# Sums moved into adding DMAs: seven weight pairs a layer and five squares of the MLP's norm in a two-layer decoder trunk

## The chip, the cores and the metric

The kernel runs on one core of a Trainium2 chip. The metric is the device time of one execution in microseconds. The engines are named as in the profile: PE (TensorE: matmuls, with its weight loads listed as PEld), DVE (VectorE), ACT (ScalarE), POOL (GpSimd) and SP (SyncE, which here issues DMAs and nothing else). A `q` behind an engine's name is its queue, the part that waits and issues.

## The reference

A trunk of two layers on 512 tokens of width 1024, in float32. Cut to what matters here:

```python
def hybrid_layer(x, g_mix, w_in, sinks, w_a, w_b, w_out, g_mlp, w_up, w_down):
    h = rmsnorm(x, g_mix)
    z = h @ w_in
    ...
    ya = sliding_window_sink_attention(aq, ak, av, sinks) @ w_a
    ...
    yb = r.astype(x.dtype) @ w_b
    mixed = jax.nn.sigmoid(ga) * ya + jax.nn.sigmoid(gb) * yb
    x = x + mixed @ w_out
    h2 = rmsnorm(x, g_mlp)
    x = x + jnp.square(jax.nn.relu(h2 @ w_up)) @ w_down
    return x
```

`rmsnorm` divides by the root of the mean of the squares over the 1024 features. `r` is the output of a retention with four heads. A last norm follows the second layer.

## The kernel before

**Layout.** Activations are kept transposed: features on the 128 partitions, the 512 tokens along the free dimension, so a tensor of width 1024 is eight tiles of 128 x 512. The residual `x` stays in SBUF as such eight tiles.

**Three matmuls for one.** PE multiplies in a reduced float32 format. To keep the precision each operand is split into a high part (ACT copies it into the format, L255 for weights, L308 and L311 for activations) and a low part (DVE subtracts the high part, L256, L309, L312). A product is then high by high, high by low and low by high (`products`, L301 to L303; `wide_pair` puts two of them into one matmul of 512 columns, L1259, and the third into L1260).

**Weights.** They come from DRAM in units of 128 x 1024 in one fixed order (`unit_order`). `load_until` issues the loads on SP's queue into `raw` tiles, of which there are three; `split_until` makes the high and low halves, three of each; `unit` hands them to the matmuls and keeps the splitting three units ahead of PE. A load waits until its `raw` tile is free.

**Pairs.** Most of `w_b`, `w_out` and `w_up` is multiplied in a form with seven block products in place of eight, in the manner of Strassen and Winograd: two units (two rows of the stacked weights, here `one` and `two`) become four parts, and parts 0 to 2 hold sums and differences of halves of 128 x 512. `load_part` issues the loads of a pair: for part 0 the left half of `one` (L210) and all of `two` (L212, into the `raw` tile that later serves part 3), for part 1 the right half of `one` (L215). `add_part` forms the sums on DVE: for part 0 the right half becomes the sum of the two halves of `two` (L221), for part 1 L224, for part 2 L228 and L229. The activations get the same treatment (`sum_input`, L559 to L563). A layer has 19 pairs: two in `w_b`, three in `w_out`, fourteen in `w_up`. `narrow_pair` multiplies with 256 columns a matmul and moves partial sums with ACT (L595, L598, L602); `wide_pair` is used for `w_up` from unit 6 on.

**The norm of the MLP.** In the out-projection the first two tiles of `x` come from `two_chunks`, the other six from three pairs. When a tile is done, `next_input` scales and splits it (L311, L312) and adds its squares up (`squared_input`, `square_sum`): the first square goes straight into the accumulator `acc` (L391), each of the seven that follow is made by ACT in a temporary (L394) and added by DVE (L395). Temporaries of that tag are six. During the first group of `w_up` the sum is split (`sum_parts`, the tiles `sh` and `sl`), multiplied with ones on PE (L430) and turned into the factor `rstd` (L431, L432), which the results of `w_up` are multiplied with.

**Order.** Each engine works through its instructions in a fixed order. The order is planned when the program is built, by a scheduler that goes through the code's order and lets an instruction pass that cannot start yet by its own model of time; a few places fix the order by hand (`issue_after`). Where instructions fall away or come in, the plan is made anew.

Of the kernel before, what the change touches and what calls it, by code (L numbers as in the profile page):

```python
# [13 lines left out]
AF = mybir.ActivationFunctionType  # L14
ALU = mybir.AluOpType
# [6 lines left out]
KD = D // P  # L22
# [35 lines left out]
def unit_order():  # L58

    def plain(name, *at):  # L60
        return [(name, i) for i in range(*at)]

    def pairs(src, *firsts):
        return [("pair", j, part, src) for j in firsts for part in range(4)]

    order = plain("w_in", 26) + plain("w_a", 4) + plain("w_in", 26, 46)
    order += pairs("w_b", 0, 2) + plain("w_b", 4, 8)
    order += plain("w_out", 2) + pairs("w_out", 2, 4, 6)
    for what, q, i in mlp_sequence():
        if what == "first":  # L70
            order += plain("w_up", 4)
        elif what == "pair":
            order += pairs("w_up", 8 * q + 2 * i)
        elif what == "down":
            order += plain("w_down", 8 * q + 2 * i, 8 * q + 2 * i + 2)
        else:
            order += plain("w_down", 8 * q, 8 * q + 8)
    return order
# [48 lines left out]
def decoder(ctx, tc, xT, x_first, w_in, w_a, w_b, w_out, w_up, w_down, tables, decay, band, triangles, g_last, out):  # L127
    nc = tc.nc
# [13 lines left out]
    def temp(name="t"):  # L142
        return tmp.tile([P, T], F32, tag="t", name=name)

    def big(name, dtype=F32):
        return tmp.tile([P, 2, T], dtype, tag="big", name=name, bufs=7)
# [13 lines left out]
    x = little_x[:, P:].rearrange("p (k t) -> p k t", t=T)  # L160
# [4 lines left out]
    order = [(layer, *u) for layer in range(DEPTH) for u in unit_order()]  # L165
    raws, parts, homes = {}, {}, []
# [8 lines left out]
    def raw_tile():  # L175
        return wpool.tile([P, UNIT], F32, tag="raw", name="raw")
# [8 lines left out]
    def load_until(n):  # L185
        while state["loaded"] < min(n, len(order)):
            i = state["loaded"]
            layer, name, j = order[i][:3]
            if name == "pair":
                load_part(i)  # L190
            else:
                raws[i] = raw_tile()
                for at in halves(i):
                    queue = nc.scalar if i == 0 and at.start == 0 else nc.sync
                    queue.dma_start(raws[i][:, at], weights[name][layer, j][:, at])
                    if i < 3:
                        load_x()
            state["loaded"] += 1
# [3 lines left out]

    LEFT, RIGHT = slice(0, UNIT // 2), slice(UNIT // 2, UNIT)

    def load_part(i):
        layer, _, j, part, src = order[i]
        one, two = (weights[src][layer, j + a] for a in range(2))
        if part == 0:
            raws[i] = raw_tile()
            nc.sync.dma_start(raws[i][:, LEFT], one[:, LEFT])  # L210
            raws[i + 3] = raw_tile()
            nc.sync.dma_start(raws[i + 3], two)  # L212
        elif part == 1:
            raws[i] = big("raw2").rearrange("p a t -> p (a t)")
            nc.sync.dma_start(raws[i][:, RIGHT], one[:, RIGHT])  # L215

    def add_part(i):
        part = order[i][3]
        if part == 0:
            w2 = raws[i + 3]  # L220
            nc.vector.tensor_tensor(raws[i][:, RIGHT], w2[:, RIGHT], w2[:, LEFT], ALU.add)  # L221
        elif part == 1:
            w1 = raws[i - 1]
            nc.vector.tensor_tensor(raws[i][:, LEFT], w1[:, RIGHT], w1[:, LEFT], ALU.subtract)  # L224
        elif part == 2:
            raws[i] = big("raw3").rearrange("p a t -> p (a t)")
            w1, w2, z2 = raws[i - 2], raws[i + 1], raws[i - 1]
            nc.vector.tensor_tensor(raws[i][:, LEFT], w1[:, LEFT], w2[:, RIGHT], ALU.subtract)  # L228
            nc.vector.tensor_tensor(raws[i][:, RIGHT], z2[:, RIGHT], z2[:, LEFT], ALU.subtract)  # L229

    def split_until(n):
        while state["split"] < min(n, len(order)):
            i = state["split"]
            load_until(i + 3)
            paired = order[i][1] == "pair"
            if paired:
                add_part(i)
            raw = raws[i]
            if homes and i >= len(order) - len(homes):
                home = homes[len(order) - 1 - i]  # L240
                hi, lo = (home[:, 2 * a : 2 * a + 2, :].rearrange("p a t -> p (a t)") for a in range(2))
            else:


                first = (ASIDE, ASIDE) if paired else (0, 0)
                if paired and order[i][4] == "w_up" and wide(order[i][2]):
                    first = (ASIDE, 0)
                hi, lo = (
                    wpool.tile([P, UNIT + P], F32R, tag=n, name=n)[:, a : a + UNIT] for n, a in zip(("hi", "lo"), first)
                )  # L250
            for at in (LEFT,) if paired and order[i][3] == 3 else halves(i):
                if i == 0 and at.start == 0:
                    nc.vector.tensor_copy(hi[:, at], raw[:, at])
                else:
                    nc.scalar.activation(hi[:, at], raw[:, at], AF.Copy)  # L255
                last_low[:] = [nc.vector.tensor_tensor(lo[:, at], raw[:, at], f32(hi[:, at]), ALU.subtract).ins]  # L256
            raws.pop(i - 3 if paired else i, None)
            parts[i] = (hi, lo)
            state["split"] += 1
# [129 lines left out]
    def square_sum(acc, src, first):  # L389
        if first:  # L390
            nc.scalar.activation(acc, src, AF.Square)  # L391
        else:
            sq = temp("sq")
            nc.scalar.activation(sq, src, AF.Square)  # L394
            nc.vector.tensor_tensor(acc, acc, sq, ALU.add)  # L395
# [38 lines left out]
    acc_of = {}  # L434

    def scaled_input(k, which):

        split(*xs[k], x[:, k, :], gain[:, which * KD + k : which * KD + k + 1])

    def squared_input(k, which):  # L440
        if k == 0:
            acc_of[which] = tmp.tile([P, T], F32, tag="acc", name="acc", bufs=1)
        square_sum(acc_of[which], x[:, k, :], k == 0)

    class Rms:

# [89 lines left out]
    def layer_body(layer):  # L536
        g_mix, g_mlp = 2 * layer, 2 * layer + 1
# [116 lines left out]
        def squares():  # L654
            for k in range(KD):
                squared_input(k, g_mix)
# [420 lines left out]
        for u in range(4):  # L1077
            hi, lo = unit("w_a", layer)
            for j in range(2):
                c = 2 * u + j  # L1080
# [103 lines left out]

        def next_input(c):
            scaled_input(c, g_mlp)
            squared_input(c, g_mlp)

        def put_x(c):
            def put(ps):  # L1190
                nc.vector.tensor_tensor(x[:, c, :], x[:, c, :], ps, ALU.add)
                next_input(c)

            return put
# [15 lines left out]
        for c in range(2, KD, 2):  # L1210
            pool = ps_mm if c == 4 else ps_aux
            narrow_pair(pool, lambda ins: None, form_of(by_form_m), block_m, add_to_x(c))
            for i in range(2):
                next_input(c + i)
# [122 lines left out]
        def put_down(c, last=False):  # L1337
            def put(ps):
                nc.vector.tensor_tensor(x[:, c, :], x[:, c, :], ps, ALU.add)  # L1339
                if last:  # L1340
                    scaled_input(c, g_mix + 2)
                    squared_input(c, g_mix + 2)
                    nc.sync.dma_start(spill[:, c, :], x[:, c, :])

            return put
# [216 lines left out]
```

## Time and profile before

| | |
|---|---|
| median of 3 runs | 1479.97 us (1479.74 to 1479.98) |
| the profiled execution | 1481.1 us, its span 1478.5 us |
| mean granted PE clock | 0.999 |
| DMA | 166.13 MB, mean 112 GB/s, queue of SP 34.9% of 16 engines' span |
| L395, adds of squares | 28 instructions of 685 ns |
| L394, squares | 28 instructions of 619 ns |

The span runs from the first to the last instruction; what lies around it in the profiled execution is 1481.1 - 1478.5 = 2.6 us. A row of a timeline gives the start and the duration in us, the engine, the line, the operation, the tile written and those read, the shapes, and in brackets the idle time before it and what ended it. A row of a group gives the count, the busy time, the mean of one in ns and the idle time before. Weight units are used in this order within layer 0: `w_b` from about 319 us, `w_out` from 360, `w_up` from 404; layer 1 does the same 732 us later.

### The profile page before, as it was taken

What the parts mean: (1) busy time and instruction counts of PE and PEld (TensorE: products, weight loads), DVE (VectorE), ACT (ScalarE), POOL (GpSimd) and SP (SyncE); (2) the same over time, 40 slices, a digit from 0 to 9 for tenths busy, and PEclk for the clock granted to TensorE, in tenths of its full rate; (3) what the DMA queues carried; (4) which work ended last, traced back from release to release, by engine and by line L of the source; (5) the groups of instructions that cost most, each with busy time, mean ns of one, the idle gap of its engine ahead of it and who ended that gap; (6) DMA issues with size and microseconds to landing.
All of it is one profiled execution on the core that took longest, in us unless ns stands there. A gap on an engine that the chain in (4) does not pass through costs nothing.

```text
span 1478.5 us, 20008 instructions
## 1 busy us (share of the span) xinstructions
PE 1467.9 (99%) x7466; PEld 1249.9 (85%) x7466; DVE 1162.7 (79%) x1920; ACT 810.3 (55%) x1302; POOL 3.8 (0%) x14
## 2 busy tenths in 40 slices
PE   9999999999999999999999999999999999999998
PEld 7888888888988888888888888888889888888887
DVE  7998668778998787776678975686889977878763
ACT  7656356654674445444556743656547654444553
POOL 0000000000000000000000000000000000000000
PEclk9999999999999999999999999999999999999999
DMA  6422223246323333333543232323553323333241
GB/s 226 135 87 86 93 82 104 93 164 191 102 79 114 100 114 94 106 100 115 170 128 91 85 98 89 99 92 98 175 167 104 101 97 99 115 101 112 89 141 57
DMA packets 56945, 166.13 MB, mean 112 GB/s; under 512 B 6896, under 2 KB 7056, under 8 KB 56848
## 3 DMA queue, kind: packets, MB, share of 16 engines
q1 hardware_dynamic: 56560, 164.33, 34.9%
q8 instruction: 58, 0.95, 0.3%
q10 hardware_dynamic: 288, 0.52, 0.1%
q14 instruction: 39, 0.32, 0.1%
HBM read 153.80 MB, written 8.40 MB: 110 GB/s over the span
## 4 chain that ended last, share of the span: by engine, by line
PE 86%; DVE 6%; issue 6%; DMA 1%; ACT 0%; POOLq 0%; DVEq 0%; SPq 0%
PE mm L303 20%; PE mm L301 20%; PE mm L302 20%; PE mm L1259 10%; PE mm L1260 5%; DVE lo L256 2%; PE rv L301 2%; PE rv L302 2%; PE rv L303 2%; DVE r L309 1%; PE score L797 1%; PE r L301 1%; PE r L303 1%; PE r L302 1%; DMA inv<-row 0%
## 5 line engine op out<-in xcount | busy, mean ns | idle before, releaser
L302 PE MATMUL mm<-r,hi 128*128 128x512 f32 (+1 forms) x1568 | 572.7, 367 | 0.0
L301 PE MATMUL mm<-r,hi 128*128 128x512 f32 (+1 forms) x1568 | 570.6, 368 | 1.4 <-ACT eu L598 0.7
L303 PE MATMUL mm<-r,lo 128*128 128x512 f32 (+1 forms) x1568 | 563.1, 367 | 1.6 <-DVE lo L256 1.3
L255 ACT ACTIVATE hi<-raw 128x1024 fp32r<-128x1024 f32 (+1 forms) x334 | 334.4, 1003 | 393.1 <-PE mm L302 210.9
L256 DVE TENSOR_TENSOR lo<-raw,hi 128x512 fp32r<-128x512 f32 (+1 forms) x335 | 385.2, 1152 | 118.8 <-ACT hi L255 115.7
L303 PEld LDWEIGHTS mm<-r,lo 128*128 128x128 f32 x1568 | 293.3, 188 | 51.1 <-DVE lo L256 3.7
L301 PEld LDWEIGHTS mm<-r,hi 128*128 128x128 f32 x1568 | 294.0, 188 | 50.2 <-ACT eu L598 1.5
L302 PEld LDWEIGHTS mm<-r,hi 128*128 128x128 f32 x1568 | 294.3, 188 | 45.7
L1259 PE MATMUL mm<-r,hi 128*128 128x512 f32 x728 | 251.9, 391 | 0.0
L1260 PE MATMUL mm<-r,lo 128*128 128x256 f32 x728 | 200.4, 277 | 1.2 <-DVE lo L256 1.1
L1259 PEld LDWEIGHTS mm<-r,hi 128*128 128x128 f32 x728 | 136.5, 188 | 28.3
L1260 PEld LDWEIGHTS mm<-r,lo 128*128 128x128 f32 x728 | 136.6, 188 | 5.2 <-DVE lo L256 2.7
L1339 DVE TENSOR_TENSOR x<-x,mm 128x512 f32<-128x512 f32 x56 | 37.8, 687 | 29.2 <-PE mm L303 29.2
L1332 ACT ACTIVATE z<-z 128x512 f32<-128x512 f32 x56 | 32.5, 624 | 48.3 <-DVE z L1312 48.3
L302 PE MATMUL rv<-lo,r 128*128 128x512 f32 x128 | 49.8, 389 | 0.0
L303 PE MATMUL rv<-hi,r 128*128 128x512 f32 x128 | 49.5, 389 | 0.0
L301 PE MATMUL rv<-hi,r 128*128 128x512 f32 x128 | 49.4, 390 | 0.0
L308 ACT ACTIVATE r<-z 128x512 fp32r<-128x512 f32 x64 | 38.7, 621 | 12.6 <-DVE z L1022 12.5
L309 DVE TENSOR_TENSOR r<-z,r 128x512 fp32r<-128x512 f32 x64 | 43.1, 686 | 2.8 <-ACT r L308 2.6
L824 ACT ACTIVATE sm<-sm,st 128x256 f32<-128x256 f32 (+1 forms) x64 | 30.2, 474 | 19.1 <-DVE st L812 18.9
L1312 DVE SCALAR_TENSOR_TENSOR z<-z,rstd 128x512 f32<-128x512 f32 x52 | 35.7, 687 | 0.6
L221 DVE TENSOR_TENSOR raw<-raw 128x512 f32<-128x512 f32 x38 | 26.0, 684 | 7.0 <-DMA raw<-w_up_in 6.3
(261 smaller groups left out, 1693.0 us busy)
## 6 DMA issues: line engine op xcount, KB each, us to landing
raw<-w_in_in SPq DMA_DIRECT2D x89, 512.0 KB, 3.6
raw<-w_down_in SPq DMA_DIRECT2D x64, 512.0 KB, 3.6
raw<-w_up_in SPq DMA_DIRECT2D x36, 512.0 KB, 3.6
raw<-w_up_in SPq DMA_DIRECT2D x56, 256.0 KB, 2.8
raw<-w_b_in SPq DMA_DIRECT2D x12, 512.0 KB, 4.0
raw<-w_out_in SPq DMA_DIRECT2D x10, 512.0 KB, 7.1
raw<-w_a_in SPq DMA_DIRECT2D x8, 512.0 KB, 3.5
aside<-gb SPq DMA_DIRECT2D x8, 512.0 KB, 4.7
```

Source lines behind the costliest of these rows:

```text
L255: nc.scalar.activation(hi[:, at], raw[:, at], AF.Copy)
L256: last_low[:] = [nc.vector.tensor_tensor(lo[:, at], raw[:, at], f32(hi[:, at]), ALU.subtract).ins]
L301: nc.tensor.matmul(ps, ah, bh, start=start and i == 0, stop=False, **more)
L302: nc.tensor.matmul(ps, ah, bl, start=False, stop=False, **more)
L303: nc.tensor.matmul(ps, al, bh, start=False, stop=stop and i == n - 1, **more)
L308: nc.scalar.activation(hi, src, AF.Copy)
L309: nc.vector.tensor_tensor(lo, src, f32(hi), ALU.subtract)
L1259: nc.tensor.matmul(both, hi[:, c], m, start=start and k == 0, stop=False, **more)
L1260: nc.tensor.matmul(ps[:, :H], lo[:, c], m[:, 0, :], start=False, stop=k == 3 and start, **more)
L1312: nc.vector.scalar_tensor_tensor(z[:, :, at], z[:, :, at], 0.0, factor, ALU.max, ALU.mult)
L1332: nc.scalar.activation(z[:, i, :], z[:, i, :], AF.Square)
L1339: nc.vector.tensor_tensor(x[:, c, :], x[:, c, :], ps, ALU.add)
```

## The change

In `load_part` a pair is `summed` when it belongs to `w_b` or `w_out`, or to `w_up` with a first unit below 8: two, three and two, seven a layer. For a summed pair SP loads the right half of `two` into the right half of part 0's tile as well, and POOL then issues a DMA that loads the left half of `two` and adds it to what is there. `add_part` does nothing for part 0 of such a pair. All of `two` is loaded as before, for parts 2 and 3.

For the MLP's norm the squares of tiles 1 to 5 are made by ACT as before and added to `acc` by DMAs that POOL issues, from SBUF to SBUF. The square of tile 6 is kept, the square of tile 7 is added to it by DVE, and that sum to `acc`.

```diff
+    def summed(i):
+
+        _, _, j, _, src = order[i]
+        return src != "w_up" or j < 8
+
     def load_part(i):
         layer, _, j, part, src = order[i]
         one, two = (weights[src][layer, j + a] for a in range(2))
@@
             nc.sync.dma_start(raws[i][:, LEFT], one[:, LEFT])
             raws[i + 3] = raw_tile()
             nc.sync.dma_start(raws[i + 3], two)
+            if summed(i):
+                nc.sync.dma_start(raws[i][:, RIGHT], two[:, RIGHT])
+                nc.gpsimd.dma_start(raws[i][:, RIGHT], two[:, LEFT], accum_op=ALU.add)
         elif part == 1:
             raws[i] = big("raw2").rearrange("p a t -> p (a t)")
             nc.sync.dma_start(raws[i][:, RIGHT], one[:, RIGHT])
@@ def add_part(i):
         if part == 0:
             w2 = raws[i + 3]
+            if summed(i):
+                return
             nc.vector.tensor_tensor(raws[i][:, RIGHT], w2[:, RIGHT], w2[:, LEFT], ALU.add)
@@
-    def squared_input(k, which):
+    def squared_input(k, which, by_dma=False):
         if k == 0:
             acc_of[which] = tmp.tile([P, T], F32, tag="acc", name="acc", bufs=1)
-        square_sum(acc_of[which], x[:, k, :], k == 0)
+        acc = acc_of[which]
+        if not by_dma or k == 0:
+            square_sum(acc, x[:, k, :], k == 0)
+        elif k < KD - 2:
+            sq = temp("sq")
+            nc.scalar.activation(sq, x[:, k, :], AF.Square)
+            nc.gpsimd.dma_start(acc, sq, accum_op=ALU.add)
+        elif k == KD - 2:
+            acc_of["last"] = temp("sq")
+            nc.scalar.activation(acc_of["last"], x[:, k, :], AF.Square)
+        else:
+            last = acc_of.pop("last")
+            square_sum(last, x[:, k, :], False)
+            nc.vector.tensor_tensor(acc, acc, last, ALU.add)
@@
         def next_input(c):
             scaled_input(c, g_mlp)
-            squared_input(c, g_mlp)
+            squared_input(c, g_mlp, True)
```

## The prediction

> **What bounds the kernel now.** I read the page first, for the engine that sets the time.
>
> ```profile
> span 1478.5 us, 20008 instructions
> ...
> PE 1467.9 (99%) x7466; PEld 1249.9 (85%) x7466; DVE 1162.7 (79%) x1920; ACT 810.3 (55%) x1302; POOL 3.8 (0%) x14
> ...
> PE 86%; DVE 6%; issue 6%; DMA 1%; ACT 0%; POOLq 0%; DVEq 0%; SPq 0%
> ```
>
> TensorE (PE) is busy for 99% of the span. VectorE (DVE) has 79% and only 6% of the chain that ended last, but that share may sit in one place, and the change takes work from DVE alone. So the second view is the busy time of each engine by stretches, over the part of layer 0 in which the edited lines run (the sum also holds the same five stretches of layer 1, 732 us later).
>
> ```profile
> 300.00:340.00 40.00, 39.72 (x249) 35.52 (x248) 34.52 (x50) 23.05 (x34) 0.00 (x0) 1.00 0.52 171
> 340.00:380.00 40.00, 39.63 (x211) 34.08 (x211) 36.03 (x49) 19.24 (x26) 0.00 (x0) 1.00 0.53 171
> 380.00:400.00 20.00, 19.33 (x162) 18.90 (x160) 19.43 (x31) 13.20 (x22) 0.00 (x0) 1.00 0.26 80
> ...
> 430.00:450.00 20.00, 19.39 (x118) 16.63 (x118) 19.71 (x34) 14.12 (x23) 0.00 (x0) 1.00 0.34 108
> ...
> sum 300.00, PE 295.79 PEld 261.91 DVE 276.88 ACT 181.90 POOL 0.00; mean PE 29.58 PEld 26.19 DVE 27.69 ACT 18.19 POOL 0.00
> ```
>
> The columns are PE, PEld, DVE, ACT and POOL busy, the granted clock, the DMA share and GB/s. From 380 to 400 and from 430 to 450 DVE is as full as PE (19.43 and 19.71 of 20), and PE has its holes there. All holes of both layers together are 300.00 - 295.79 = 4.21 us. Who PE waits for, over the whole span:
>
> ```profile
> PE mm L303 <- DVE lo L256: 1.3, 2, 0.7
> PE mm L1260 <- DVE lo L256: 1.1, 3, 0.5
> ...
> PE mm L301 <- ACT eu L598: 0.7, 2, 0.4
> PE mm L301 <- ACT eu L602: 0.5, 2, 0.3
> ```
>
> So what can be won is a few us: waits for the low half of a weight unit (DVE), and waits for ACT, which the change does not relieve. The sizes here are too small, because the modelled end of a matmul covers part of each wait. The starts in PE's timeline give the full price:
>
> ```profile
> 337.38 0.40 PE L301 MATMUL mm<-r,hi 128*128 128x512 f32 x1
> 337.62 0.40 PE L302 MATMUL mm<-r,hi 128*128 128x512 f32 x1
> 338.10 0.50 PE L303 MATMUL mm<-r,lo 128*128 128x512 f32 x1
> ...
> 391.12 0.28 PE L301 MATMUL mm<-r,hi 128*128 128x256 f32 x1
> 391.23 0.28 PE L302 MATMUL mm<-r,hi 128*128 128x256 f32 x1
> 392.18 0.38 PE L303 MATMUL mm<-r,lo 128*128 128x256 f32 x1 [0.67 <-DVE lo L256]
> 392.40 0.28 PE L301 MATMUL mm<-r,hi 128*128 128x256 f32 x1
> ...
> 434.29 0.40 PE L1259 MATMUL mm<-r,hi 128*128 128x512 f32 x1
> 435.16 0.38 PE L1260 MATMUL mm<-r,lo 128*128 128x256 f32 x1 [0.47 <-DVE lo L256]
> ```
>
> A 256-wide matmul is followed after 0.11 us (391.12 to 391.23), a 512-wide one after 0.24 (337.38 to 337.62). So the stop at 391 costs 392.18 - 391.23 - 0.11 = 0.84, and 0.11 more as the next start is also late (392.40): 0.95. The stop at 434 costs 435.16 - 434.29 - 0.24 = 0.63, with the same aftermath 0.74. The stop at 337 costs 0.24 and 0.11: 0.35. These three are what DVE makes PE lose; each opens with the matmul that needs a low half.
>
> **What the change removes.** Seven pairs a layer lose the DVE add of part 0 (L221), five squares a layer lose theirs (L395). The last two squares keep two adds between them, as before.
>
> ```profile
> L221 DVE TENSOR_TENSOR raw<-raw 128x512 f32<-128x512 f32 x38 | 26.0, 684 | 7.0 <-DMA raw<-w_up_in 6.3
> ...
> L395 DVE TENSOR_TENSOR acc<-acc,sq 128x512 f32<-128x512 f32 x28 | 19.2, 685 | 0.0
> ```
>
> That is 24 instructions of 0.68 us, 16.4 us of DVE in the program. What counts is where they stand in DVE's order ahead of the three stops:
>
> ```profile
> 325.39 0.69 DVE L221 TENSOR_TENSOR raw<-raw 128x512 f32<-128x512 f32 x1
> ...
> 386.24 0.69 DVE L221 TENSOR_TENSOR raw<-raw 128x512 f32<-128x512 f32 x1
> ...
> 387.50 0.69 DVE L395 TENSOR_TENSOR acc<-acc,sq 128x512 f32<-128x512 f32 x1
> ...
> 390.30 0.69 DVE L395 TENSOR_TENSOR acc<-acc,sq 128x512 f32<-128x512 f32 x1
> 390.91 1.22 DVE L256 TENSOR_TENSOR lo<-raw,hi 128x1024 fp32r<-128x1024 f32 x1
> ...
> 428.87 0.63 DVE L221 TENSOR_TENSOR raw<-raw 128x512 f32<-128x512 f32 x1
> ```
>
> An add holds DVE's next instruction back by 0.61 us (390.30 to 390.91). The stop at 391 waits for the low half begun at 390.91. Three of the removed adds stand directly ahead of it, 1.83 us. Its other input, the high half, comes from ACT:
>
> ```profile
> 388.29 1.06 ACT L255 ACTIVATE hi<-raw 128x1024 fp32r<-128x1024 f32 x1
> ```
>
> It ends at 389.35, so the low half can begin 1.56 us earlier, more than the 0.95 of the stop: all of it goes. Ahead of the stop at 434 DVE has no gap from the reciprocal (it ends as L221 begins at 428.87) and one removed add: 0.6 of the 0.74 goes. Ahead of the stop at 337 one removed add, at 325.39, in a run of DVE without a gap longer than 0.5: all of 0.35. Sum: 0.95 + 0.6 + 0.35 = 1.9 us a layer, **3.8 us** in both.
>
> **What it adds.** Per pair, SP issues one 256 KB load more (the right half of the second row), and POOL then issues a 256 KB load that adds onto it. Per square, POOL issues a 256 KB transfer from SBUF to SBUF that adds onto the running sum. POOL has nothing else to do (14 instructions). The new wait stands on POOL's queue: an adding transfer waits until the right half has landed, or until the sum before it has, and behind it wait only other adding transfers. The trace shows no adding transfer and none issued by POOL. From issue to landing call it A. The nearest rows are the ordinary loads by SP, first of the page, then of the tensor w_out in the crowded stretch:
>
> ```profile
> raw<-w_up_in SPq DMA_DIRECT2D x56, 256.0 KB, 2.8
> ...
> DMA to landing us min/median/max: 3.2/7.2/7.3
> ```
>
> From below A is 2.8, one ordinary load. From above 14.6: twice 7.3, since an adding transfer reads two things, each as slowly as the slowest row. Nothing excludes the far end, but none of the waits falls in the crowded stretch except w_out's first pair, so I take 5.6, twice the ordinary load. [...]
>
> Where must it land? The tightest pair is the third of w_out, whose loads SP issued like this:
>
> ```profile
> 376.92 0.33 SPq L210 DMA_DIRECT2D raw<-w_out_in  x1
> 377.30 0.42 SPq L215 DMA_DIRECT2D raw<-w_out_in  x1
> 382.35 0.33 SPq L212 DMA_DIRECT2D raw<-w_out_in  x1
> ```
>
> L212, the whole second row, stands before L215 in the program and yet was issued after it, because it needs a buffer that comes free later. So SP's order lets work pass a load without a buffer, and the new load, which writes the same buffer as L210, should go out at 377.3 and land at 380.1. Without any stop at 391 the high half has to begin by 388.9 (0.95 before 390.91, less its own 1.06). So A may be 8.8, and 5.6 fits. The sum also no longer waits for L212's row. The extra traffic, 0.5 MB a pair, meets a DMA share of 0.53 at most, and PE's holes were not in the stretch where it is highest.
>
> The squares form a chain, since each must wait for the one before:
>
> ```profile
> 398.25 0.62 ACT L394 ACTIVATE sq<-x 128x512 f32<-128x512 f32 x1
> ...
> 414.97 0.68 DVE L395 TENSOR_TENSOR acc<-acc,sq 128x512 f32<-128x512 f32 x1
> ...
> 421.51 0.39 PE L430 MATMUL ssq<-sh,ones 128*128 128x512 f32 x1
> ```
>
> Four of the five come between ACT's squares ahead of 387.50 and the one that ends at 398.87. With A of 5.6 the second to fifth end no later than 398.87 + 2 x 5.6 = 410.1, before the final add at 414.97. The last two squares now make two adds in a row there, 0.61 longer; PE asks for the sum at 421.51, and between lie only the split's copy and one subtraction (some 2 us), so it is hidden. If the chain ran to 419.5, that cover would be gone. Squares stay on ACT, and their buffers are held longer, at most three of the six of that tag at once.
>
> **Sum.** The profiled span 1478.5 less 3.8 is 1474.7. Around the span lay 2.6 us (the profiled execution took 1481.1), so 1477.3 for an execution like it; the median of the three runs, 1479.97, lies 1.1 below that execution, so **1476.2**.
>
> **Rivals.** *More than the three stops.* With DVE freer, ACT's work moves forward too, and the waits for eu go as well. For it: DVE is nearly full wherever PE has holes. The ceiling is the 4.21 us of holes, plus 0.27 that each of about 18 stops hides behind the modelled ends and in the late start after it: 9 us. Against it: ACT's burst of squares and scalings is not touched. With two thirds of the ceiling, 6 us: 1474.
>
> *The gain is hidden or given back.* The order on each engine is planned anew when instructions fall away, and a stop filled at 391 may open elsewhere: PE has nothing to spare at 99%. For it: the stops are all under 1 us, so one instruction ordered otherwise costs as much as was won. With half of it lost: 1478; with all, 1480. [...]
>
> *The adding transfers land too late: slower.* One mechanism, the chain of squares in the out-projection. Its second to fifth link start no earlier than 386.2 (the add of the second ran at 387.50) and end at 386.2 + 4 A. It decides from A = (419.5 - 386.2) / 4 = 8.3 on, and every us of A above that stops PE for 4 us in each layer, since the matmul with ones at 421.51 holds all of PE's queue. At A = 10 that is 6.7 a layer, 13 in all, less what is won elsewhere, 3: 1490. The same point decides for the pair at 391 (8.8). For it: two reads for one write, and the w_out rows of 7.2. Against it: 2.8 in the uncrowded stretch, where this chain runs (DMA share 0.26).
>
> *The right half's load goes out behind L212 and not before.* Then it lands at 382.7 + 2.8 = 385.5, only 3.4 remain for A, and with 5.6 the stop at 391 is 2.2 long in place of 0.95. Against it speaks the order of L215. 1480 to 1482; I count it to the given-back cases.
>
> **How the numbers follow.** Chances: forecast 0.52 (its own range 1474 to 1478.5), more 0.10, hidden or given back 0.23, too late 0.15. About 0.2%, 3.0 us, is what a measurement of this kernel can tell from no change. Faster by more than that means under 1477.0: all of *more* and 0.40 of the forecast, 0.50. Slower, over 1482.9: all of *too late* and 0.02 of the given-back cases, 0.17. Within: 0.33. The range from 1473 to 1482 leaves out most of *too late* and the best part of *more*.
>
> **What would show it.** Right: L221 counts 24, L395 with the new add 18, DVE busy near 1146; POOL issues 24 transfers that land in under 8 us; the stops at 337 and 391 are gone in both layers and the one at 434 is below 0.2; the new load is issued next to L210. Wrong: PE waits at the matmul with ones or for a high half that waits for a POOL transfer (too late); DVE instructions longer than 0.69 beside POOL's issues (held); three stops gone and new ones of the same size elsewhere (given back).

## The result and the profile after

The changed kernel takes 1499.97 us (median of 4 runs, 1498.68 to 1501.05), the kernel before, timed beside it, 1479.89 (1479.74 to 1479.98). The ratio is 1.0135, with a 95% interval from 1.0118 to 1.0153: **20.1 us slower**. The forecast was 1476.2 with a range to 1482.

Line numbers are those of the changed kernel from here on. L265 is ACT's copy of a weight unit to its high half and L266 DVE's low half (L255 and L256 before); L311 to L313 are the three products (L301 to L303 before), L319 makes the low half of an activation, L322 that of a tile of `x`, and L618, L621 and L625 are ACT's copies of partial sums (L595, L598 and L602 before).

The page of the changed kernel, with the busy time of the engines, the chain that ended last by engine, and one costly group:

```profile
span 1499.3 us, 20085 instructions
...
PE 1474.6 (98%) x7466; PEld 1254.2 (84%) x7466; DVE 1150.0 (77%) x1896; ACT 809.3 (54%) x1302; POOL 24.7 (2%) x38
...
PE 80%; DVE 7%; issue 7%; DMA 5%; ACT 1%; SPq 0%; POOLq 0%; DVEq 0%
...
L234 DVE TENSOR_TENSOR raw<-raw 128x512 f32<-128x512 f32 x38 | 26.1, 687 | 22.6 <-DMA raw<-w_out_in 12.0
```

DVE lost the 24 instructions (1920 to 1896) and 12.7 us of work. What is new is the share of DMA in the chain, 1% before and 5% now, and the last row. L234 is the subtraction that makes part 1 of a pair (L224 before, with no idle time ahead of it). It reads both halves of part 0's tile, the sum among them, and DVE now stands idle 22.6 us ahead of it. Two lists of waits show the same from both ends. First, the waits of DVE and ACT for a load of weights that POOL had part in (engine, line, what it waited for: us in total, times, longest):

```profile
ACT hi L265 <- DMA raw<-w_out_in: 12.1, 2, 6.1
DVE raw L234 <- DMA raw<-w_out_in: 12.0, 4, 3.5
...
DVE raw L234 <- DMA raw<-w_up_in: 10.4, 4, 3.7
```

Second, what PE waited for:

```profile
PE mm L311 <- ACT eu L621: 6.4, 5, 2.4
PE ssq L440 <- DVE sl L319: 5.0, 2, 2.7
PE mm L313 <- DVE lo L266: 2.1, 3, 1.0
PE mm L1282 <- ACT hi L265: 1.8, 2, 0.9
```

No row of PE's waits names a DMA: PE waits for ACT's copies and for the split of the norm's sum, and the two largest rows are traced below to what stands in a queue behind the waiting subtraction. The busy time in the stretches that the prediction looked at (PE, PEld, DVE, ACT, POOL, granted clock, DMA share, GB/s):

```profile
380.00:400.00 20.00, 17.56 (x146) 17.36 (x147) 16.50 (x26) 11.80 (x20) 3.89 (x5) 1.00 0.73 171
...
430.00:450.00 20.00, 16.81 (x111) 15.58 (x110) 18.50 (x24) 13.42 (x23) 0.00 (x0) 0.91 0.18 58
```

From 380 to 400 DVE fell from 19.43 to 16.50, as was meant, but PE fell with it, from 19.33 to 17.56. This is that place in the changed kernel, from SP's, POOL's, DVE's, ACT's and PE's timelines in turn, for the third pair of `w_out`:

```profile
379.98 0.33 SPq L215 DMA_DIRECT2D raw<-w_out_in  x1
380.36 0.42 SPq L219 DMA_DIRECT2D raw<-w_out_in  x1
```

```profile
384.66 0.86 POOL L220 DMA_DIRECT2D raw<-w_out_in  x1 [3.46 <-DVE raw L238]
```

```profile
385.63 1.22 DVE L266 TENSOR_TENSOR lo<-raw,hi 128x1024 fp32r<-128x1024 f32 x1
389.98 0.69 DVE L234 TENSOR_TENSOR raw<-raw 128x512 f32<-128x512 f32 x1 [3.13 <-DMA raw<-w_out_in]
390.59 0.41 DVE L1222 TENSOR_TENSOR x<-x,mm 128x256 f32<-128x256 f32 x1
```

```profile
391.03 0.72 ACT L321 ACTIVATE r<-x 128x512 fp32r<-128x512 f32 x1 [2.57 <-DVE x L1222]
...
392.18 0.36 ACT L621 ACTIVATE eu<-mm 128x256 f32<-128x256 f32 x1
```

```profile
390.23 0.28 PE L313 MATMUL mm<-r,lo 128*128 128x256 f32 x1
392.60 0.38 PE L311 MATMUL mm<-r,hi 128*128 128x256 f32 x1 [2.08 <-ACT eu L621]
```

SP issues the left half of the first row at 379.98 and the right half of the second next to it. The right half lands 3.7 us after its issue, at 384.03 by the trace, and POOL issues its adding load 0.6 later, at 384.66 (its row names DVE's L238, but 0.6 to 0.7 us lie between the right half's landing and POOL's issue in the other pairs too). The sum lands just ahead of 389.98: ten microseconds from the pair's first load to the sum, since the two transfers come one after the other. DVE reaches L234 over three microseconds earlier and waits. Behind L234 stands the add that completes a tile of `x` (L1222); ACT stands still 2.57 us for that tile with the copy L621 queued behind; PE needs the copy. The stop at PE is 392.60 - 390.23 - 0.12 = 2.25 us, where the stop at 391 had cost 0.95.

In `w_up` the second pair meets the norm. POOL, DVE and PE:

```profile
425.65 0.87 POOL L220 DMA_DIRECT2D raw<-w_up_in  x1 [12.02 <-DVE lo L266]
```

```profile
431.41 0.69 DVE L234 TENSOR_TENSOR raw<-raw 128x512 f32<-128x512 f32 x1 [2.25 <-DMA raw<-w_up_in]
432.02 0.69 DVE L319 TENSOR_TENSOR sl<-acc,sh 128x512 fp32r<-128x512 f32 x1
```

```profile
430.21 0.28 PE L313 MATMUL mm<-r,lo 128*128 128x256 f32 x1
432.76 0.70 PE L440 MATMUL ssq<-sl,ones 128*128 128x512 f32 x1 [2.28 <-DVE sl L319]
433.25 0.42 PE L311 MATMUL mm<-r,hi 128*128 128x256 f32 x1
433.47 0.42 PE L312 MATMUL mm<-r,hi 128*128 128x256 f32 x1
```

Here L234 holds `sl`, and the matmul with ones that reads `sl` holds all of PE's queue: 432.76 - 430.21 - 0.12 = 2.43 us. Behind it the matmuls start 0.22 us apart and not 0.12 (the last two rows); that is told at the end.

Were the transfers slow? The source views of L220 and L459 give the time from issue to landing, of the adding loads and of the adds of squares:

```profile
DMA to landing us min/median/max: 4.0/5.2/7.0
```

```profile
DMA to landing us min/median/max: 3.3/4.1/6.6
```

They were not: the forecast had taken 5.6. The adding loads from DRAM took a median of 5.2 us, the adds inside SBUF 4.1.

If every start of a matmul is compared with the usual distance for its width, the delays over 0.02 us add up to 16.1 us in the trace of before and 36.9 in that of after. The 20.8 of difference are the whole result, and all of them lie in 320 to 480 and 1060 to 1220, where the seven pairs and the squares are. The four stops behind a waiting L234, at the third pair of `w_out` and at the norm, are 2.25 and 2.43 us in layer 0 and 2.59 and 2.91 in layer 1, 10.2 us together. A lower clock behind the two stops of the norm adds some 4.8, worked out at the end. The rest is smaller stops, among them 0.99 at 325 and at 1066, which e13 explains in part.

### The profile page after: what moved, and what is told of

Read it like the earlier page. It is cut to its first block, busy times and chain, and to the rows that moved or that the text cites. A ratio compares the mean times of both kernels' runs of the same rounds, so it can differ in the third digit from the quotient of the medians.

```text
span 1499.3 us, 20085 instructions
## 1 busy us (share of the span) xinstructions
PE 1474.6 (98%) x7466; PEld 1254.2 (84%) x7466; DVE 1150.0 (77%) x1896; ACT 809.3 (54%) x1302; POOL 24.7 (2%) x38
## 4 chain that ended last, share of the span: by engine, by line
PE 80%; DVE 7%; issue 7%; DMA 5%; ACT 1%; SPq 0%; POOLq 0%; DVEq 0%
PE mm L311 18%; PE mm L313 18%; PE mm L312 18%; PE mm L1282 9%; PE mm L1283 5%; DMA raw<-w_out_in 2%; DVE lo L266 2%; PE rv L311 2%; PE rv L312 2%; PE rv L313 2%; DMA raw<-w_up_in 2%; DVE r L319 1%; PE score L820 1%; PE r L311 1%; PE r L313 1%
## 5 line engine op out<-in xcount | busy, mean ns | idle before, releaser
L311 PE MATMUL mm<-r,hi 128*128 128x512 f32 (+1 forms) x1568 | 573.5, 369 | 8.4 <-ACT eu L621 6.4
L313 PE MATMUL mm<-r,lo 128*128 128x512 f32 (+1 forms) x1568 | 565.6, 368 | 2.2 <-DVE lo L266 2.1
L265 ACT ACTIVATE hi<-raw 128x1024 fp32r<-128x1024 f32 (+1 forms) x334 | 333.5, 1002 | 393.8 <-PE mm L312 208.7
L266 DVE TENSOR_TENSOR lo<-raw,hi 128x512 fp32r<-128x512 f32 (+1 forms) x335 | 384.5, 1151 | 116.5 <-ACT hi L265 112.2
L311 PEld LDWEIGHTS mm<-r,hi 128*128 128x128 f32 x1568 | 296.2, 189 | 57.8 <-ACT eu L621 7.8
L313 PEld LDWEIGHTS mm<-r,lo 128*128 128x128 f32 x1568 | 295.1, 189 | 52.0 <-DVE lo L266 5.1
L313 PE MATMUL rv<-hi,r 128*128 128x512 f32 x128 | 49.5, 389 | 0.0
L311 PE MATMUL rv<-hi,r 128*128 128x512 f32 x128 | 49.4, 390 | 0.0
L319 DVE TENSOR_TENSOR r<-z,r 128x512 fp32r<-128x512 f32 x64 | 42.8, 685 | 7.1 <-ACT r L318 7.1
L234 DVE TENSOR_TENSOR raw<-raw 128x512 f32<-128x512 f32 x38 | 26.1, 687 | 22.6 <-DMA raw<-w_out_in 12.0
```

The lines of the kernel that those rows point to most:

```text
L311: nc.tensor.matmul(ps, ah, bh, start=start and i == 0, stop=False, **more)
L313: nc.tensor.matmul(ps, al, bh, start=False, stop=stop and i == n - 1, **more)
L319: nc.vector.tensor_tensor(lo, src, f32(hi), ALU.subtract)
```

## The experiments

All were timed against the kernel before, in the same batches. Line numbers are those of each kernel, which differ by one or two from the changed kernel's. The first question was which part costs the time, and whether the blocked reader is the cause.

**e1: the pairs alone** (the squares as before).

```diff
-            squared_input(c, g_mlp, True)
+            squared_input(c, g_mlp)
```

> The sums of the seven pairs a layer by adding DMAs, the squares as before. Theory (the reader blocks: DVE's subtraction for part 1 and ACT's high half of part 0 stand in their engines' fixed orders ahead of the landing of the sum, which comes 10 us after the first load of the pair was issued, and hold all that is queued behind them): most of the loss stays, 1490 to 1500 us, with DVE waiting over 20 us in total for the loads of w_out and w_up ahead of that subtraction. Rival (the chain of squares costs it): 1480 or less. Rival (POOL's issues hold DVE): in between, with DVE adds longer than 0.69 us.

Measured: 1493.18 us (1492.22 to 1494.92), ratio 1.0094 [1.0079, 1.0109], 13.6 us slower. The waits for weights in its trace:

```profile
ACT hi L265 <- DMA raw<-w_out_in: 11.9, 2, 6.2
DVE raw L234 <- DMA raw<-w_out_in: 11.4, 4, 3.1
DVE raw L234 <- DMA raw<-w_up_in: 7.9, 4, 2.5
```

They are nearly the waits of the full change; DVE's make 19.3 us, a little under the 20 that I had expected. Two thirds of the loss come with the pairs alone. DVE's adds kept their length (680 to 695 ns at L234 in the changed kernel), and its two-input instructions that ran during one of POOL's issues are no longer than the others (17 adds of 512 columns, median 686 ns both), so no holding of DVE by POOL shows.

**e2: the squares alone.**

```diff
-        return src != "w_up" or j < 8
+        return False
```

> Five squares a layer by adding DMAs, the pairs as before. Theory of the blocking reader: nothing reads the sum of squares until all are done, so no engine waits for it; 1477 to 1481 us. Rival (the chain of squares): 1490 or more, with PE waiting at the matmul with ones. Rival (any new order loses a few us, whatever it is for): 1482 to 1488.

Measured: 1482.69 (1481.82 to 1483.54), 1.0020 [1.0011, 1.0030], 3.1 slower. That is above the theory's range and in that of the second rival, a new order that loses a few us. The chain of adds is not late. PE's first wait is another:

```profile
PE mm L311 <- ACT rstd L441: 2.7, 2, 1.3
```

The matmuls write into banks of PSUM, of which the program has a pool of five (`ps_mm`) and one of three (`ps_aux`). The first pair of `w_up` needs all three of `ps_aux`, and the norm's bank stays taken until ACT has read it for `rstd`, which comes later in the new order; 1.49 us a layer by PE's starts.

**e3: the pairs without the adding load**, so that only the second transfer and its wait are gone and DVE is as free as the change makes it.

```diff
                 nc.sync.dma_start(raws[i][:, RIGHT], two[:, RIGHT])
-                nc.gpsimd.dma_start(raws[i][:, RIGHT], two[:, LEFT], accum_op=ALU.add)
```

> Pairs alone, and the adding DMA itself left out (the right half of part 0 then holds half of the sum); the load of the right half by SP stays. Squares as before. Theory of the blocking reader: one landing instead of two, so the wait goes; 1474 to 1479 us, which is what the removed adds are worth. Rival (the new order or the extra load loses the time): 1485 or more.

Measured: 1478.86 (1478.35 to 1479.85), 0.9996 [0.9986, 1.0006]. So the adds of the pairs, removed for nothing, gain 0.7 us, and by the interval that cannot be told from zero. The stops at 337 and 391 are gone in its trace and the one at 434 is down to 0.4; but the stop at `rstd` is there too, and one for a copy of ACT, 0.36 and 0.45 before, has grown to 0.99 and 0.90:

```profile
PE mm L310 <- ACT rstd L440: 2.7, 2, 1.3
PE mm L310 <- ACT eu L624: 1.6, 2, 0.8
```

**e4: one landing in place of two.** POOL issues its load, but as a plain one, and SP's load of the right half is left out.

```diff
-                nc.sync.dma_start(raws[i][:, RIGHT], two[:, RIGHT])
-                nc.gpsimd.dma_start(raws[i][:, RIGHT], two[:, LEFT], accum_op=ALU.add)
+                nc.gpsimd.dma_start(raws[i][:, RIGHT], two[:, LEFT])
```

> Pairs alone, and in place of the load by SP and the adding DMA one plain load by POOL (the right half of part 0 then holds half of the sum). Squares as before. Theory (two landings in a row are too late, one is not): within 3 us of the kernel without the add. Rival (the path by POOL is slow in itself, whatever it waits for): near the kernel with pairs alone, 1488 or more.

Measured: 1479.07 (1478.32 to 1480.80), 0.9998 [0.9989, 1.0007]. This is the sharpest comparison: against e1 the planned order is nearly the same (all but 20 of DVE's 1906 instructions stand in the same sequence, all but 4 of ACT's 1302 and all but 6 of PE's 7466), POOL issues the same number of transfers, and 14 us are gone. Among the 20 is the subtraction itself, and it stands earlier here than in e1, not later. The third pair of `w_out`, first in e1, then in e4:

```profile
384.40 0.68 DVE L1222 TENSOR_TENSOR x<-x,z 128x512 f32<-128x512 f32 x1
...
389.27 0.69 DVE L234 TENSOR_TENSOR raw<-raw 128x512 f32<-128x512 f32 x1 [3.05 <-DMA raw<-w_out_in]
```

```profile
382.38 0.69 DVE L233 TENSOR_TENSOR raw<-raw 128x512 f32<-128x512 f32 x1
382.98 0.69 DVE L1221 TENSOR_TENSOR x<-x,z 128x512 f32<-128x512 f32 x1
```

No engine waits for POOL's loads in e4. So the 14 us lie hardly in the order, and neither in the way through POOL's queue nor, by e3, in the extra load by SP. What remains is the sum that lands second.

**e5 and e6: the norm's bank.** If the stop at `rstd` is what eats the gain of e3, a bank of another pool should give it back. The edit, on e3 (e5) and on the kernel before (e6):

```diff
-        ps = bank(ps_aux, "ssq")
+        ps = bank(ps_mm if len(both) == 2 else ps_aux, "ssq")
```

> The kernel without the add (the right half of part 0 holds half of the sum), with one edit more: the bank for the norm's sum comes from the pool of five, one of which is free then, and not from the pool of three that the first pair of w_up wants whole. Theory (the three DVE stops are gone there, and a new stop of 1.5 us a layer, PE waiting for ACT's rstd to give that bank back, eats the gain): the new stop goes, 1475 to 1477 us. Rival (the removed adds are worth nothing, the stops move about): 1478.5 to 1480.

> The kernel before with the bank edit alone. It has no stop at that place, so theory: 1479 to 1480 us. Rival (the bank edit is worth something by itself): under 1478.

Measured: e5 1479.06 (0.9996 [0.9986, 1.0006]), e6 1480.12 (1.0002 [0.9993, 1.0011]). The stop at `rstd` is gone from e5, and the time is not:

```profile
PE mm L1282 <- DVE lo L265: 2.7, 2, 1.4
```

A low half now comes late; the reciprocal of the norm (3.35 us on DVE) stands ahead of it. My theory missed and its rival fits: the stop moved by a few us and kept its size (1.53 by PE's starts). The bank edit alone (e6) is worth nothing, as expected.

**e7: the late reader.** The full change, with the subtraction of part 1 placed by hand behind the last low half, so that DVE comes to it later.

```diff
-            nc.vector.tensor_tensor(raws[i][:, LEFT], w1[:, RIGHT], w1[:, LEFT], ALU.subtract)
+            with tc.issue_after(last_low[0]) if summed(i - 1) else ExitStack():
+                nc.vector.tensor_tensor(raws[i][:, LEFT], w1[:, RIGHT], w1[:, LEFT], ALU.subtract)
```

> The whole change, with DVE's subtraction for part 1 of a summed pair held behind the low half of part 0 in DVE's order. The transfers are the same. Theory (that subtraction waits for the sum's landing at the head of DVE's queue, and holds the work behind it): most of the loss goes, 1480 to 1488 us, and the waits of DVE for the sum's landing ahead of it fall from 22 us to under 5. Rival (the landing itself is too late for the matmuls): 1495 or more.

Measured: 1487.23 (1485.49 to 1489.21), 1.0051 [1.0036, 1.0066]. That is 12.7 of the 20.1 us back. No wait of DVE for a sum is left. ACT's is, since the high half of part 0 reads the sum as well:

```profile
ACT hi L266 <- DMA raw<-w_out_in: 10.4, 3, 5.0
```

**e8: the same transfers, unread.** e3, with a load and an adding load into a spare tile that nothing reads, to price the traffic by itself. The tiles of the halves were made shorter for room.

```diff
+                nc.sync.dma_start(spare, two[:, 512:992])
+                nc.gpsimd.dma_start(spare, two[:, 0:480], accum_op=ALU.add)
```

> The kernel without the add (the right half of part 0 holds half of the sum), and beside it, for each of the fourteen pairs, a load by SP and an adding DMA by POOL into a spare tile of 480 columns that nothing reads. [...] Theory of the blocking reader: 1478 to 1480.5 us, as without them. [...]

Measured: 1516.97, 1.0252 [1.0237, 1.0267]. It does not answer its question. Since the transfers depend on nothing, the plan put them all into the first 150 us, where attention's own moves then came late: from 50 to 150 us PE ran 422 matmuls, 486 in the kernel before. And matmuls of 512 columns took 394 to 396 ns and not 391 throughout, with the tiles moved. By the usual distance of their starts the 5274 matmuls of that width came 4 ns later each, 231 ns after the one before and not 227, which makes 21 us. Whether the shorter tiles are the cause was not tried. What the extra traffic costs at its own place was not tried in another way; that e4, with one load less and nothing to wait for behind it, is as fast as the kernel before, and that no adding load took over 7.0 us, speaks against much.

**e9 and e10: the price of the hold.** e9 is e1 with the hold of e7, e10 the kernel before with the same hold.

> The pairs by adding DMAs with DVE's subtraction for part 1 held behind the low half of part 0, the squares as before. Theory of the blocking reader: against 1493.2 us without the hold most of the loss goes; what is left is ACT's wait for the sum of the first pair of w_out, 4.8 us where loads crowd: 1481 to 1485. Rival (the whole gain of the hold came from the squares' side): 1490 or more.

> The kernel before with that hold alone, for the same seven pairs a layer. Theory (the hold helps only where the sum lands late): 1479 to 1482 us. Rival (the hold makes any of these kernels faster): under 1477.

Measured: e9 1485.30 (1.0038 [1.0025, 1.0051]), e10 1482.57 (1.0019 [1.0010, 1.0029]). Both lie a little above what I had expected (up to 1485 and up to 1482). The hold takes 7.9 of the pairs' 13.6 away, though it costs 2.9 by itself. Between e9 and e10 only 2.7 remain, for the adding loads under a late reader.

**e11: the squares with the other bank** (e2 with the edit of e5).

> The squares by adding DMAs alone, with the norm's bank from the pool of five. Theory (the 3 us that the squares cost alone are the stop of 1.5 us a layer in which PE waits for that bank): 1479 to 1480.5 us. Rival (the stop moves to the next low half, as it did without the add): 1482 to 1483.

Measured: 1479.30 (1478.31 to 1479.53), 0.9995 [0.9986, 1.0005]. With the bank edit all of the 3.1 us are gone. Adding the squares up by DMA costs nothing then and brings nothing that can be measured.

**e12 to e15: the pairs by tensor.** Only the two pairs of `w_b` with the hold (e12) and without (e13), only the three of `w_out` (e14), only the two of `w_up` (e15), all without the squares.

```diff
-        return src != "w_up" or j < 8
+        return src == "w_b"
```

> Only the two pairs of w_b a layer by adding DMAs, with the hold; the squares as before. Their sums landed 8 us and more ahead of the low half that needs them. Theory: no engine waits for a sum; 1478.5 to 1481 us. Rival (any pair by this path costs about 1 us): 1483 or more.

> Adding DMAs for the two pairs of w_b a layer alone, no hold, squares as before. Theory (a pair costs where an engine is seen to wait for its sum; in w_b none is): 1479 to 1481 us. Rival (each of the seven pairs costs its share of the 13.6): 1483.5, two sevenths.

> Adding DMAs for the three pairs of w_out a layer alone, no hold, squares as before. Theory (DVE and ACT wait 23 us here, most of what they wait for sums at all): the largest share, 1485 to 1490 us. Rival (each pair its share): 1485.5, three sevenths, with the three parts equal per pair.

> Adding DMAs for the first two pairs of w_up a layer alone, no hold, squares as before. Theory (DVE waits 7.9 us here, and the work of the norm stands behind it): 1482 to 1486 us. Rival (each pair its share): 1483.5.

Measured: e12 1482.98 (1.0022 [1.0012, 1.0032]) and e13 1482.55 (1.0018 [1.0009, 1.0028]), both slower than I had expected and under a us from their rivals; e14 1487.37 (1.0047 [1.0032, 1.0062]); e15 1487.22 (1.0048 [1.0033, 1.0063]). The last is also more than expected. My theory, that a pair costs where an engine waits for its sum, is therefore not all. In e13 no engine waits for a sum at all, and yet 2.7 us are lost. DVE's order shows why. First the kernel before, then e13:

```profile
323.05 0.68 DVE L858 TENSOR_TENSOR gb<-mm,rstd 128x512 f32<-128x512 f32 x1
...
326.32 0.69 DVE L224 TENSOR_TENSOR raw<-raw 128x512 f32<-128x512 f32 x1
```

```profile
322.78 0.68 DVE L234 TENSOR_TENSOR raw<-raw 128x512 f32<-128x512 f32 x1
323.38 1.22 DVE L319 TENSOR_TENSOR r<-sums,r 128x1024 fp32r<-128x1024 f32 x1
324.51 0.69 DVE L881 TENSOR_TENSOR gb<-mm,rstd 128x512 f32<-128x512 f32 x1
```

```profile
326.19 0.39 PE L311 MATMUL mm<-r,hi 128*128 128x256 f32 x1 [0.82 <-ACT eu L625]
```

The subtraction stood three microseconds behind the product `gb` and now stands ahead of it, since the plan makes the sum ready without DVE. `gb` runs later, ACT works on it before the copy L625, and PE waits. By PE's starts 1.8 us are lost between 320 and 340 where 0.8 had been, and 3.0 between 1040 and 1060 where 1.4 had been: nearly all of the 2.7. This was read from the trace and not tried by itself; e12, in which the hold puts the subtraction back behind `gb`, loses about as much, most of it at another place (1.23 at 377.6 where 0.53 had been). The three parts make 2.7 + 7.5 + 7.4 = 17.6, and e1, which has them all, 13.6: e13 and e15 keep the stop at 391 that e1's other pairs remove (0.84 a layer), and e13 and e14 keep the one at 434.

**e16: late reader and other bank** (e7 with the edit of e5).

> The whole change with both repairs: the hold and the bank edit. Theory (the bank's stop of 1.5 us a layer shows only where the norm's sum is not late itself; with the hold the norm came on time): 1484 to 1487 us against 1487.2 with the hold alone; what is left is ACT's wait in w_out, which neither repair touches. Rival (both repairs together bring it back): 1481 or less.

Measured: 1486.07 (1485.38 to 1487.24), 1.0043 [1.0026, 1.0060]. That is within the expectation. The best form of the full change is still 6 us behind the kernel before. None of the versions beats it by more than a measurement can tell.

## Why the prediction was wrong

**The step that failed** is the sentence on what the change adds: "The new wait stands on POOL's queue ... and behind it wait only other adding transfers." It followed the transfer to its landing and asked when the high half of part 0 must begin. It did not list who reads the sum, so the time that other engines wait for it stood at nothing in the forecast. Besides the low half, which follows the high half, there are two readers, the high half on ACT and the subtraction of part 1 on DVE, and either holds all that its engine has queued behind it. For the pair at 391 the time that I had worked out for the high half even sufficed: counted from the pair's first load, the high half had to begin 12.0 us later (388.9 - 376.9), and the sum took 10.0. The other reader came first, DVE waited 3.13 us, and the add of `x` behind it was what PE lacked. The rival in which the right half's load goes out late gave 2.2 us for this stop, near the 2.25 measured, but by chance: that load did go out next to the pair's first. e1 shows that these waits come with the pairs, e4 that they and 14 us go when the sum lands first and not second, e7 and e9 that a later reader gets 12.7 and 7.9 us back.

**The size of A was right**, 5.2 and 4.1 us against 5.6, and so was the order of the new load, issued at 380.36 next to L215 at 379.98. The right half ahead of it was in the forecast with 2.8 us and took a median 3.7, and POOL's issue came 0.6 later. So the third pair's sum was there 9.6 us after the right half's load was issued, where the forecast had 8.4 (2.8 and 5.6). That is a matter of size; what the forecast left out is that DVE, which had made the sum in 0.7 us of its own time, now stands still until it lands.

**The gain of 3.8 us was the second wrong term.** The three stops went nearly as forecast: e3 and e4 are without those at 337 and 391, and the one at 434 fell to 0.39, where 0.14 had been forecast. Yet both are worth 0.7 and 0.5 us against the kernel before of the same batch, which their intervals do not tell from zero. The rival *given back* is what happened to this part of the sum: the order was planned anew, and stops at `rstd` (1.49 a layer) and at a copy of ACT (0.99) took their place. When the first was removed (e5) another of its size opened. I had priced that rival at a chance of 0.23 and the forecast at 0.52; after these runs I would put them the other way round.

**The rival that ended slower had the right sign and the wrong mechanism.** The chain of squares was never late: POOL issued its last link at 404.19, with no landing over 6.6 us, and the final add on DVE ran at 425.60. The matmul with ones did wait, but for `sl` behind the subtraction of a pair. In the kernel before, `sl` stood ahead of the subtractions of both summed pairs of `w_up`:

```profile
418.58 0.69 DVE L309 TENSOR_TENSOR sl<-acc,sh 128x512 fp32r<-128x512 f32 x1
...
420.31 0.69 DVE L224 TENSOR_TENSOR raw<-raw 128x512 f32<-128x512 f32 x1
```

The second pair's followed at 432.35. In the new order `sl` (432.02) stands behind both (416.78 and 431.41).

**The counts** came as forecast: L231 has 24 instructions, the adds of squares with the new one are 18 (14, 2 and 2), POOL issues 14 and 10 transfers, DVE's busy time is 1150.0 against 1146.

**The sum.** The pairs cost 13.6, the squares 3.1, together 20.1. They do not simply add: the stop at `rstd` of e1 and e2 is absent from the full change, and in its place stands the one at the matmul with ones, 2.43 and 2.91 us, each with a stretch of slow clock. It takes both parts of the change: in e1 `sl` (427.58) still stands ahead of the second pair's subtraction (431.76), and in the full change, where the last add of its input runs later (425.60 against 422.83), it stands behind. What stays open is the price of the new order by itself: e13 suggests 2.7 for `w_b`, and in e3 and e4 such losses and the stops that are gone cancel. Whether the waits would go if the loads of a pair were issued earlier was not tried.

## What to carry to other kernels

Before work is moved from an engine to a DMA, list every instruction that reads the result and where it stands in its engine's order: an engine that works in order passes the lateness on to all that is queued behind, though nothing else needs the result (here DVE's wait of 3.13 us at L234 became a stop of PE of 2.25). A load and an adding load in series need the lead of both, here ten us in place of one add of 0.7. Here, with PE busy for 99%, relieving DVE moved the stops more than it removed them: e3 and e4, with the adds of the pairs off DVE, gained 0.7 and 0.5 us where 3.8 had been forecast for the whole change. So half or all of such a gain should be counted as given back until a version with the work simply left out shows otherwise.

## What the runs showed of the hardware

A stop of PE cost more than its length, at times. Windows of 3.6 us behind four stops of the changed kernel, the two of the third pair and the two of the norm, and one that follows the last (PE, PEld, DVE, ACT, POOL, then the granted clock, DMA share, GB/s):

```profile
392.60:396.20 3.60, 3.60 (x30) 3.60 (x31) 3.60 (x8) 1.74 (x3) 0.84 (x1) 1.00 0.65 85
432.80:436.40 3.60, 3.60 (x16) 3.51 (x17) 3.60 (x3) 0.69 (x1) 0.00 (x0) 0.53 0.00 0
1133.20:1136.80 3.60, 3.53 (x29) 3.53 (x30) 3.60 (x8) 1.74 (x4) 0.86 (x1) 1.00 0.62 76
1174.20:1177.80 3.60, 3.57 (x15) 3.48 (x16) 3.60 (x3) 0.69 (x1) 0.00 (x0) 0.50 0.00 0
1177.00:1180.40 3.40, 3.40 (x18) 3.40 (x18) 3.37 (x2) 0.43 (x1) 0.00 (x0) 0.50 0.00 0
```

After the norm's stops (2.43 us at 430.21, 2.91 at 1171.20) the clock was granted at 0.53 and 0.50 and PE ran 16 and 15 matmuls where it runs 30. The trace's record of the clock has half speed from 432.89 for 3.41 us, and from 1173.58 for 6.83, twice as long. The first cost some 1.7 us (half of 3.41), the second some 3.1 (half of what lay behind the stop's end at 1174.23). After the third pair's stops (2.25 and 2.59 us) it was granted in full. In e1 it is the third pair's stops, 2.28 and 2.29 us, that half speed follows, for 3.41 us each. The length does not decide between them. e14 has it at the third pair, after a stop of 2.34 us in layer 0 and not after one of 2.39 in layer 1:

```profile
391.00:394.60 3.60, 3.51 (x16) 3.41 (x17) 3.60 (x6) 1.26 (x3) 0.00 (x0) 0.56 0.29 71
1126.20:1129.80 3.60, 3.51 (x26) 3.22 (x26) 3.60 (x6) 1.37 (x3) 0.00 (x0) 1.00 0.29 82
```

Half speed followed six stops of the changed kernel, e1, e14 and e15, of 2.22 us (e15) to 2.91, and did not follow five others of 2.14 to 2.59. What decides it no run shows.
